# Sample state updates of a retention layer: 32-row stationary tiles replaced by one zero-padded operand of 128 rows

## The chip, the cores and the metric

The kernel runs on one core of a Trainium2 chip. The metric is device time in microseconds (us) of one execution, as the median of several runs. The profile is one execution that was recorded by the hardware profiler; its own time is given beside those of the runs.

## What is computed

The program is one inference step of a two-layer decoder trunk, for 1024 prompt tokens and for 64 sample tokens (8 sequences of 8), which share the weights. Layer 0 mixes tokens by sliding-window attention, layer 1 by retention, a linear attention with a state of 256 x 512 numbers per head and sequence. The change lies in the retention of the sample tokens:

```
def retention_chunk(state, q, k, v, lg):
    ...
    inner = jnp.einsum('bhqs,bshe->bqhe', a, v)
    cross = jnp.einsum('bqhd,bhde->bqhe', q, state) * jnp.exp((idx + 1.0)[:, None] * lg[None])[None, :, :, None]
    k_dec = k * jnp.exp((L - 1.0 - idx)[:, None] * lg[None])[None, :, :, None]
    new_state = jnp.exp(L * lg)[None, :, None, None] * state + jnp.einsum('bshd,bshe->bhde', k_dec, v)
    return new_state, inner + cross
```

For the samples L is 8, there are 8 sequences b and 4 heads h, and `new_state` is an output (`srs`). The last einsum is the state update: for each sequence, head and half of the 256 key rows, a product of 8 tokens deep with 128 x 512 results.

## The kernel before

**Matrix products.** All products run in a type of 32 bits that TensorE takes at reduced precision (`F32R`); where that is not enough, an operand is split into a high and a low part and the product is made as hi x hi, hi x lo and lo x hi. The large projections are made by `mm_t` (L135 to L137, stationary weights, 384 or 320 columns at a time) and `group_n` (L194 to L196, stationary activations, 256 columns). They form a nearly unbroken stream on TensorE. Weights come in slots of 128 x 1024 through a buffer `wraw` (two of them, loaded by SP's queue at L107), and ScalarE and VectorE split them into `whi` and `wlo` (L281, L282).

**Retention of layer 1.** `layer1` weaves the projections with a generator, `ret_units`. It goes through 4 heads x 8 chunks of the prompt. In the round of a chunk stand, one after the other: `ret_mid` of that chunk, `ret_sample_step` with the chunk's number i (0 to 7) as its step, `ret_gate` of the chunk before, `ret_in` of the next chunk, and `ret_sample_load` for the next step. So each head has 8 sample steps. Step i works on the group g = i // 4 of four sequences, on the half k = i // 2 % 2 of the key rows, and on two of the four sequences j (0 and 1 in even steps, 2 and 3 in odd ones).

**The sample's operands.** `ret_sample_in` writes keys and values of a head to two DRAM buffers, `s_kk` and `s_vv`, for each sequence as four blocks of 8 rows: keys hi, hi, lo, lo and values hi, lo, hi, lo. 32 rows of one sequence multiplied with each other so give all four products of the split at once. `ret_sample_load` fetches in even steps four state tiles `s0`, and where k is 0 also the four sequences' keys, as one tile of 128 x 256 from the pool tag `kh1`, and their values, as `vst1` of 128 x 512, one buffer. Both are then used in four steps.

**The update.** `ret_sample_step` makes, for its two sequences, a matmul on the 32 partitions of sequence j (L1080, keys stationary with 32 rows, values moving with 512 columns) into a PSUM buffer `pa` (four in all). VectorE adds the decayed state (L1083) and POOL's queue stores the result (L1084). That makes 4 heads x 8 steps x 2 = 64 such matmuls. In even steps four matmuls come ahead of them for each half (L1069, stationary operands of 128 rows and 32 columns), and in step 0 three with 64 rows (L1072 to L1074).

**What sets the order.** The program's text says what depends on what; the framework replays it in a simulated schedule and writes one list of instructions for each engine, which that engine then takes strictly in turn. Only `weave` with its rates says how densely `ret_units` stands between the projections. SP's queue has the loads, POOL's queue the stores.

Of the kernel before, what the change touches and what calls it, by code (L numbers as in the profile page):

```python
# [9 lines left out]
F32 = mybir.dt.float32  # L10
F32R = mybir.dt.float32r
AF = mybir.ActivationFunctionType
ALU = mybir.AluOpType
# [3 lines left out]
P = 128  # L17
# [36 lines left out]
class Trunk:  # L54
# [795 lines left out]
    def ret_const(self, pool):  # L850
        nc = self.nc
        self.rdec = pool.tile([P, 6, 4], F32, name="rdec", bufs=1)
        nc.sync.dma_start(self.rdec, self.io["rdec"])
        self.qpad = pool.tile([P, 2, 2, 4, 32], F32, name="qpad", bufs=1)
        nc.gpsimd.memset(self.qpad, 0.0)
        self.asamp = [pool.tile([TS, P], F32R, name=f"asamp{i}", bufs=1) for i in range(2)]
        for a in self.asamp:
            nc.gpsimd.memset(a.bitcast(F32), 0.0)
# [181 lines left out]

    def ret_sample_load(self, pool, h, i, u):

        nc = self.nc
        if i % 2:
            return
        g, k = i // 4, i // 2 % 2
        u["s0"] = []
        for j in range(4):
            s0 = pool.tile([P, 512], F32, name="s0", bufs=8)
            nc.sync.dma_start(s0, self.io["st0"][4 * g + j, h, k * P:(k + 1) * P, :])  # L1050
            u["s0"].append(s0)
        if k == 0:
            b = 4 * g
            u["ks"] = pool.tile([P, 256], F32R, name="kh1", bufs=2)
            u["vs"] = pool.tile([P, 512], F32R, name="vst1", bufs=1)
            nc.sync.dma_start(u["ks"].bitcast(F32), self.s_kk[h, b:b + 4].rearrange("b j l c -> (b j l) c"))
            nc.sync.dma_start(u["vs"].bitcast(F32), self.s_vv[h, b:b + 4].rearrange("b j l c -> (b j l) c"))

    def ret_sample_step(self, pool, h, i, u):
        nc = self.nc  # L1060
        mm = nc.tensor.matmul
        gam = 1.0 - 2.0 ** (-5.0 - h)
        g, k = i // 4, i // 2 % 2
        if i == 0:
            u["o"] = self.pa.tile([P, 512], F32, name="pa")
        po = u["o"]
        if i % 2 == 0:
            for j in range(4):
                mm(po[32 * j:32 * j + 32], self.qpad[:, k, g, j], u["s0"][j], start=i == 0, stop=i == 6)  # L1069
        if i == 0:  # L1070
            (ah, al), (vh, vl) = u["a"], u["v"]
            mm(po, ah, vh, start=False, stop=False)  # L1072
            mm(po, ah, vl, start=False, stop=False)
            mm(po, al, vh, start=False, stop=False)  # L1074
        pair = range(i % 2 * 2, i % 2 * 2 + 2)
        pds = {}
        for j in pair:
            pds[j] = self.pa.tile([P, 512], F32, name="pa")
            r = slice(32 * j, 32 * j + 32)
            mm(pds[j], u["ks"][r, k * P:(k + 1) * P], u["vs"][r], start=True, stop=True)  # L1080
        for j in pair:
            s0 = u["s0"][j]
            nc.vector.scalar_tensor_tensor(out=s0, in0=s0, scalar=float(gam ** 8), in1=pds[j], op0=ALU.mult, op1=ALU.add)  # L1083
            nc.gpsimd.dma_start(self.io["srs"][4 * g + j, h, k * P:(k + 1) * P, :], s0)  # L1084
        if i == 7:
            u["on"] = self.groupnorm(pool, po, P, h, 4)
# [257 lines left out]
```

## Time and profile before

| | |
|---|---|
| median of 3 runs | 1697.99 us (1696.72 to 1701.69) |
| profiled execution, own time | 1695.23 us |
| its span | 1693.5 us |
| PE (matmul) busy | 1668.0 us, 98% of the span |
| PEld (weight load) busy | 1583.5 us, 94% |
| DVE (VectorE) busy | 988.7 us, 58% |
| ACT (ScalarE) busy | 612.7 us, 36% |
| POOL (GpSimd) busy | 340.0 us, 20% |
| granted TensorE clock | 0.999 of full speed |

Matmuls are pipelined: the duration of one includes the way through the array, so that the time from start to start says what one takes from the stream, and busy PE is not PE at its peak. A row of the timeline may stand for several instructions (xN) that started together or in one run. The retention's rounds lie between about 690 and 1490 us of the span.

### The profile page before, as it was taken

Reading aid. Unit: us, or ns where it says so; the run is one execution under the profiler, and the core shown is the slowest. Engines: PE = TensorE matmul, PEld = TensorE weight load, DVE = VectorE, ACT = ScalarE, POOL = GpSimd, SP = SyncE. Lnnn points to the kernel's source line nnn. Section 1 sums busy time; section 2 is a strip of 40 time slices with the busy share of each in tenths; the row PEclk is TensorE's granted clock in tenths of the full one; section 3 lists DMA queues with packets and bytes.
Section 4 is the critical chain, followed back from the end, with each engine's and each line's share of the span. In section 5 each row is a group of like instructions: output and inputs, shape, how many; then the busy total and the mean of one; then the engine's idle time right before and its main releaser. Section 6 shows DMA issues by size and latency. Waiting matters only on the chain.

```text
span 1693.5 us, 28264 instructions
## 1 busy us (share of the span) xinstructions
PE 1668.0 (98%) x10600; PEld 1583.5 (94%) x10600; DVE 988.7 (58%) x2184; ACT 612.7 (36%) x1365; POOL 340.0 (20%) x533
## 2 busy tenths in 40 slices
PE   8999999999999999999999999999999999999998
PEld 7989999988999999899999999999899988999998
DVE  7558787966248574246744655455744756443852
ACT  6245555777334341222222312322222432241421
POOL 1413312132001121211123212231122222200000
PEclk9999999999999999999999999999999999999999
DMA  8655646684315443254445544465454865482342
GB/s 288 174 142 154 168 118 170 178 273 166 119 36 173 144 146 119 80 165 154 155 165 183 184 154 160 151 188 177 146 163 146 279 199 172 167 256 86 122 143 87
DMA packets 178697, 273.15 MB, mean 161 GB/s; under 512 B 29968, under 2 KB 128336, under 8 KB 178528
## 3 DMA queue, kind: packets, MB, share of 16 engines
q1 hardware_dynamic: 141152, 177.94, 35.1%
q0 software_dynamic: 37408, 93.40, 15.7%
q8 instruction: 83, 1.36, 0.3%
q14 instruction: 54, 0.44, 0.1%
HBM read 173.45 MB, written 99.68 MB: 161 GB/s over the span
## 4 chain that ended last, share of the span: by engine, by line
PE 73%; issue 1%; DMA 0%; POOL 0%; ACT 0%; DVE 0%; POOLq 0%; ACTq 0%
PE pj L135 17%; PE pj L137 17%; PE pj L136 17%; PE pj L194 3%; PE pj L195 3%; PE pj L196 3%; PE pa L1080 1%; PE pa L1069 1%; PE pa L913 1%; PE pa L1002 1%; PE pa L1003 1%; PE pa L1004 1%; PE pa L944 1%; PE pa L987 1%; PE pa L986 1%
## 5 line engine op out<-in xcount | busy, mean ns | idle before, releaser
L135 PE MATMUL pj<-act,whi 128*128 128x384 f32 (+1 forms) x2160 | 711.9, 330 | 2.3 <-ACT ys L729 1.2
L137 PE MATMUL pj<-act,wlo 128*128 128x384 f32 (+1 forms) x2160 | 707.8, 328 | 0.0
L136 PE MATMUL pj<-act,whi 128*128 128x384 f32 (+1 forms) x2160 | 707.1, 327 | 0.0
L135 PEld LDWEIGHTS pj<-act,whi 128*128 128x128 f32 x2160 | 405.8, 188 | 11.7 <-issue 6.3
L137 PEld LDWEIGHTS pj<-act,wlo 128*128 128x128 f32 x2160 | 405.6, 188 | 4.2 <-issue 3.2
L136 PEld LDWEIGHTS pj<-act,whi 128*128 128x128 f32 x2160 | 405.8, 188 | 3.6 <-issue 2.0
L281 ACT CAST whi<-wraw 128x512 fp32r<-128x512 f32 (+1 forms) x226 | 127.9, 613 | 191.5 <-PE pj L136 150.6
L282 DVE TENSOR_TENSOR wlo<-wraw,whi 128x512 fp32r<-128x512 f32 (+1 forms) x226 | 146.7, 681 | 70.7 <-ACT whi L281 70.3
L194 PE MATMUL pj<-whi,act 128*128 128x256 f32 x528 | 149.0, 286 | 1.1 <-ACT v L871 0.6
L195 PE MATMUL pj<-wlo,act 128*128 128x256 f32 x528 | 148.7, 283 | 0.0
L196 PE MATMUL pj<-whi,act 128*128 128x256 f32 x528 | 147.9, 283 | 0.0
L194 PEld LDWEIGHTS pj<-whi,act 128*128 128x128 f32 x528 | 100.1, 191 | 7.2 <-issue 3.2
L195 PEld LDWEIGHTS pj<-wlo,act 128*128 128x128 f32 x528 | 101.0, 191 | 0.8 <-issue 0.2
L196 PEld LDWEIGHTS pj<-whi,act 128*128 128x128 f32 x528 | 100.6, 191 | 0.3 <-issue 0.2
L518 ACT ACTIVATE s_sb<-s_sb,nm 128x257 f32<-128x257 f32 (+2 forms) x136 | 65.7, 488 | 33.2 <-DVE nm L515 32.6
L871 ACT ACTIVATE v<-pj,rcol 128x256 f32<-128x256 f32 x64 | 29.9, 474 | 127.7 <-PE pj L196 91.7
L330 DVE TENSOR_TENSOR rp_a<-pj,cs 128x768 f32<-128x768 f32 (+1 forms) x39 | 35.6, 912 | 63.5 <-PE pj L137 63.5
L872 POOL DMA_DIRECT2D s_v<-v x64 | 35.4, 554 | 167.8 <-ACT v L871 167.6
L340 DVE TENSOR_TENSOR rp_b<-pj,rbc 128x768 f32<-128x768 f32 (+1 forms) x36 | 32.8, 910 | 50.8 <-PE pj L137 50.7
L959 ACT ACTIVATE kh<-pa,rdec 128x256 fp32r<-128x256 f32 (+1 forms) x36 | 17.0, 473 | 114.0 <-PE pa L956 113.4
L1083 DVE SCALAR_TENSOR_TENSOR s<-s,pa 128x512 f32<-128x512 f32 x64 | 42.2, 684 | 24.5 <-PE pa L1080 24.0
L342 ACT ACTIVATE rp_a<-rp_b 128x768 f32<-128x768 f32 (+1 forms) x36 | 29.2, 810 | 73.1 <-DVE rp_b L340 73.1
(233 smaller groups left out, 2556.6 us busy)
## 6 DMA issues: line engine op xcount, KB each, us to landing
wraw<-wt SPq DMA_DIRECT2D x110, 512.0 KB, 4.4
s<-st SPq DMA_DIRECT2D x64, 256.0 KB, 3.1
srs<-s POOLq DMA_DIRECT2D x64, 256.0 KB, 2.7
act<-s_og SPq DMA_DIRECT2D x48, 192.0 KB, 3.8
qst<-s_q SPq DMA_DIRECT2D x32, 256.0 KB, 4.5
qk<-s_qk SPq DMA_DIRECT2D x32, 256.0 KB, 3.5
s_v<-v POOLq DMA_DIRECT2D x64, 128.0 KB, 2.5
vv<-s_v SPq DMA_DIRECT2D x32, 256.0 KB, 2.7
```

Of the source, the lines that this page charges most:

```text
L135: mm(ps, hi[:, sl], a[c][:, 0], start=start and i == 0, stop=False)
L136: mm(ps, hi[:, sl], a[c][:, 1], start=False, stop=False)
L137: mm(ps, lo[:, sl], a[c][:, 0], start=False, stop=stop and i == last)
L194: mm(o, hi, w[0][:, sl], start=start, stop=False)
L195: mm(o, hi, w[1][:, sl], start=False, stop=False)
L196: mm(o, lo, w[0][:, sl], start=False, stop=stop)
L281: self.nc.scalar.copy(hi, x)
L282: self.nc.vector.tensor_tensor(out=lo, in0=x, in1=hi.bitcast(F32), op=ALU.subtract)
L330: nc.vector.tensor_tensor(out=ta, in0=ps, in1=self.cs[:, 0:1, c0:c0 + n].broadcast_to([P, 2, n]), op=ALU.mult)
L518: nc.scalar.activation(s[:, h, :], s[:, h, :], AF.Exp, bias=nm[:, h, :], scale=0.125, accum_out=den[:, h:h + 1])
L872: nc.gpsimd.dma_start(self.s_v1[h, i, :, g * 256:g * 256 + 256], st)
L1083: nc.vector.scalar_tensor_tensor(out=s0, in0=s0, scalar=float(gam ** 8), in1=pds[j], op0=ALU.mult, op1=ALU.add)
```

## The change

Two lines make a tile `kpad` of four slots, 128 rows by 128 columns each, and fill it with zeros once, at the start of layer 1. Slot j receives the 32 rows of sequence j on its own partitions 32j to 32j+31; the other 96 rows stay zero. The matmul then takes the whole slot as stationary operand and all 128 rows of `vs`: rows of other sequences meet zeros. The keys are no longer loaded as one tile of 256 columns for two halves but as four loads of 32 x 128 in every even step. There is one `kpad`, so a load into a slot has to follow the matmul that read it last. The matmuls of a step are no longer written ahead of the two VectorE operations but in turn with them.

```diff
@@ ret_const
         nc.gpsimd.memset(self.qpad, 0.0)
+        self.kpad = pool.tile([P, 4, P], F32R, name="kpad", bufs=1)
+        nc.gpsimd.memset(self.kpad.bitcast(F32), 0.0)
         self.asamp = [pool.tile([TS, P], F32R, name=f"asamp{i}", bufs=1) for i in range(2)]
@@ ret_sample_load
             u["s0"].append(s0)
+        b = 4 * g
+        for j in range(4):
+            nc.sync.dma_start(self.kpad[32 * j:32 * j + 32, j].bitcast(F32),
+                              self.s_kk[h, b + j, :, :, k * P:(k + 1) * P].rearrange("j l c -> (j l) c"))
         if k == 0:
-            b = 4 * g
-            u["ks"] = pool.tile([P, 256], F32R, name="kh1", bufs=2)
             u["vs"] = pool.tile([P, 512], F32R, name="vst1", bufs=1)
-            nc.sync.dma_start(u["ks"].bitcast(F32), self.s_kk[h, b:b + 4].rearrange("b j l c -> (b j l) c"))
             nc.sync.dma_start(u["vs"].bitcast(F32), self.s_vv[h, b:b + 4].rearrange("b j l c -> (b j l) c"))
@@ ret_sample_step
-        pair = range(i % 2 * 2, i % 2 * 2 + 2)
-        pds = {}
-        for j in pair:
-            pds[j] = self.pa.tile([P, 512], F32, name="pa")
-            r = slice(32 * j, 32 * j + 32)
-            mm(pds[j], u["ks"][r, k * P:(k + 1) * P], u["vs"][r], start=True, stop=True)
-        for j in pair:
+        for j in range(i % 2 * 2, i % 2 * 2 + 2):
+            pd = self.pa.tile([P, 512], F32, name="pa")
+            mm(pd, self.kpad[:, j], u["vs"], start=True, stop=True)
             s0 = u["s0"][j]
-            nc.vector.scalar_tensor_tensor(out=s0, in0=s0, scalar=float(gam ** 8), in1=pds[j], op0=ALU.mult, op1=ALU.add)
+            nc.vector.scalar_tensor_tensor(out=s0, in0=s0, scalar=float(gam ** 8), in1=pd, op0=ALU.mult, op1=ALU.add)
             nc.gpsimd.dma_start(self.io["srs"][4 * g + j, h, k * P:(k + 1) * P, :], s0)
```

On SP's queue the loads stand in the order of the schedule. The first place is the start of head 0, behind the load of its values (`vst`); the lines of the changed kernel are two to four higher (vst L1057 is now L1061, vv L926 is L928, s L1050 is L1053). Before:

```order
L1057 DMA vst_8315<-s_vv 128x512
L107 DMA wraw<-wt 128x1024
L926 DMA vv_9039<-s_v_89 128x512
L1050 DMA s_9239<-st 128x512
L107 DMA wraw<-wt 128x1024
L1050 DMA s_9241<-st 128x512
```

Now:

```order
L1061 DMA vst_8320<-s_vv 128x512
L1057 DMA kpad<-s_kk 32x128 x2
L107 DMA wraw<-wt 128x1024
L928 DMA vv_9047<-s_v_89 128x512
L1053 DMA s_9247<-st 128x512
L107 DMA wraw<-wt 128x1024
```

Two loads into slots 0 and 1, for step 2, stand ahead of the weights; they have to follow the two matmuls of step 0. Each head has such loads in pairs: four loads at its start, that follow no matmul of their own head, and six pairs behind steps 0 to 5.

The second place is in head 2, around two loads of weights. Before:

```order
L931 DMA sgl<-s_sg_90 128x4x128
L107 DMA wraw<-wt 128x1024 x2
L1050 DMA s_12451<-st 128x512
L924 DMA qk_12141<-s_qk_88 128x4x128
L1050 DMA s_12453<-st 128x512
```

Now:

```order
L933 DMA sgl<-s_sg_90 128x4x128
L1057 DMA kpad<-s_kk 32x128
L107 DMA wraw<-wt 128x1024
L1057 DMA kpad<-s_kk 32x128
L107 DMA wraw<-wt 128x1024
L1053 DMA s_12477<-st 128x512
```

Here each load of weights stands behind a load into `kpad`. On PE the 64 matmuls of the update stand where they stood, but for a few that moved by some matmuls of the projections.

## Rows read from the trace of the kernel before

**Rows 1.** Busy time by engine, 690 to 1490 us (x instructions, clock, DMA share, GB/s).

```profile
690.00:1490.00 800.00, 796.88 (x5035) 732.99 (x5034) 433.12 (x831) 218.81 (x441) 184.08 (x285) 1.00 0.52 170
```

**Rows 2.** Instructions of line 1080 (ns min/median/max, first and last start), whole span.

```profile
L1080 PE MATMUL pa<-vst,kh x64: 489/497/501, 745.3 to 1470.3; 32*128 32x512 f32 x64
L1080 PEldq EVENT_SEMAPHORE  x8: 51/51/933, 743.0 to 1418.2; - x8
```

**Rows 3.** Timeline of PE, a lone update (start, duration; stationary rows*columns, moving shape).

```profile
972.49 0.33 PE L136 MATMUL pj<-act,whi 128*128 128x384 f32 x1
...
973.01 0.34 PE L136 MATMUL pj<-act,whi 128*128 128x384 f32 x1
973.28 0.49 PE L1080 MATMUL pa<-vst,kh 32*128 32x512 f32 x1
973.70 0.44 PE L137 MATMUL pj<-act,wlo 128*128 128x384 f32 x1
973.97 0.34 PE L135 MATMUL pj<-act,whi 128*128 128x384 f32 x1
```

**Rows 4.** Timeline of PE, 512 columns with 128 stationary rows.

```profile
1285.76 0.40 PE L1004 MATMUL pa<-vh,kl 128*128 128x512 f32 x1
...
1286.46 0.40 PE L1004 MATMUL pa<-vh,kl 128*128 128x512 f32 x1
```

**Rows 5.** Timeline of PE, two updates started together.

```profile
820.93 0.34 PE L137 MATMUL pj<-act,wlo 128*128 128x384 f32 x1
821.20 0.50 PE L1080 MATMUL pa<-vst,kh 32*128 32x512 f32 x2
821.63 0.44 PE L135 MATMUL pj<-act,whi 128*128 128x384 f32 x1
821.91 0.34 PE L136 MATMUL pj<-act,whi 128*128 128x384 f32 x1
```

**Rows 6.** Timeline of PE, matmuls of 32 columns with and without updates behind them.

```profile
795.49 1.06 PE L1069 MATMUL pa<-s,qpad 128*32 128x512 f32 x8
796.48 0.50 PE L1080 MATMUL pa<-vst,kh 32*128 32x512 f32 x2
...
797.20 0.34 PE L136 MATMUL pj<-act,whi 128*128 128x384 f32 x1
...
1195.25 1.07 PE L1069 MATMUL pa<-s,qpad 128*32 128x512 f32 x8
...
1196.53 0.34 PE L136 MATMUL pj<-act,whi 128*128 128x384 f32 x1
```

**Rows 7.** Waits of the weight loads, 690 to 1490 us (us in total, times, longest).

```profile
PEld pa L1080 <- issue: 8.1, 28, 0.8
```

**Rows 8.** Matmuls with 64 stationary rows (line by form, ns min/median/max).

```profile
L1072 PE MATMUL pa<-vh,asamp x4: 493/493/497, 744.4 to 1343.7; 64*128 64x512 f32 x4
L1073 PE MATMUL pa<-vl,asamp x4: 383/392/393, 744.7 to 1344.0; 64*128 64x512 f32 x4
```

**Rows 9.** Waits of SP's queue, 600 to 1500 us (us in total, times, longest).

```profile
SPq L1057 <- PE pa L1080: 11.1, 4, 3.4
```

**Rows 10.** Timeline of SP's queue and of ACT: loads of weights and a split.

```profile
740.36 0.32 SPq L1057 DMA_DIRECT2D vst<-s_vv  x1
747.11 0.33 SPq L107 DMA_DIRECT2D wraw<-wt  x1
...
909.75 0.33 SPq L107 DMA_DIRECT2D wraw<-wt  x1
...
931.15 0.61 ACT L281 CAST whi<-wraw 128x512 fp32r<-128x512 f32 x1
```

**Rows 11.** Landing of the eight loads of keys (line 1056).

```profile
DMA to landing us min/median/max: 1.9/3.2/4.8
```

**Rows 12.** Timeline of POOL at the start of layer 1.

```profile
622.07 0.60 POOL L855 MEMSET qpad<- 128x512 f32 x1 [2.77 <-DMA s_x<-ys]
...
625.40 1.19 POOL L239 TENSOR_TENSOR rcol<-nv,mhalf 128x3 f32<-128x3 f32 x1 [2.16 <-DVE nv L238]
```

## The prediction

> **What bounds the kernel now.** I first looked at the busy time of each engine in the stretch in which the update runs. Between 690 and 1490 us PE is busy for 796.9 of 800 us at the full granted clock, VectorE for 433 and ScalarE for 219 [rows 1]. So TensorE sets the pace there, and whatever the stream of matmuls loses or gains goes straight into the time. Busy PE does not mean that the array does useful work all the time, though, so the next view is the timeline of PE, where the distance from start to start says what a matmul takes out of the stream. The rows to look for are the 64 updates of L1080 [rows 2]. I went through all of them along the timeline: they stand in 48 groups, 32 lone ones and 16 pairs that start together.
>
> A lone update in the middle of the projections [rows 3]: the matmuls of 384 columns ahead of it follow each other at 0.173 us (972.49 to 973.01, three steps). From the last of these to the second one behind the update, 973.01 to 973.97, it takes 0.96 us. Two steps of 0.173 us belong to the projection, so the update takes 0.61 us out of the stream. The same 512 columns with 128 stationary rows follow each other at 0.233 us (1285.76 to 1286.46, three steps) [rows 4]. So about 0.38 us of each lone update is not its work but a gap. It stands on both sides: the update starts 0.27 us after its neighbour in place of 0.17, and the projection behind it needs 0.27 us to the next start in place of 0.17.
>
> A pair takes 0.98 us in the same way (820.93 to 821.91), so 0.63 us for two [rows 5]: the second update comes free.
>
> What makes the gap? The same picture shows where 64 stationary rows come in: the first matmul of that form lasts 493 ns, the next, of the same form, 392 [rows 8]. And behind the matmuls of 32 stationary columns the stream also needs longer, 1.28 us from their start to the second projection [rows 6]. The gap appears wherever the tile's form changes, and not between matmuls of one form. The weight loads of L1080 wait 28 times, 8.1 us in all, for nothing that the profile shows [rows 7], which is how a gap inside TensorE would look.
>
> **The change, part by part.**
>
> The matmuls. With 128 stationary rows the update has the form of its neighbours, and I price it at 0.233 us like the other matmuls of 512 columns [rows 4]. By groups:
> - 28 lone updates with projections on both sides: 28 x 0.38 = 10.8 us gained.
> - 6 pairs with projections on both sides: before 0.63 us, after 2 x 0.233 = 0.47, so 6 x 0.17 = 1.0 us gained.
> - 10 pairs that touch another form (32 columns, 64 rows, transposes). Behind matmuls of 32 columns, from their start to the second projection, it is 1.71 us with the pair (795.49 to 797.20); without updates it is 1.28 [rows 6]. After the change it would be 1.28 + 0.47 = 1.75: nothing gained, since the change of form stays with the neighbour. I take 0 for all ten; at best each gains like a pure pair (+1.7 us), at worst each loses the 0.04 just worked out (-0.4 us).
> - 4 lone updates that touch another form: a lone one takes as long as a pair, so 1.71 - (1.28 + 0.23) = 0.20 us each behind the 32 columns, and at most 0.38 each. I take 0.28: 1.1 us gained.
>
> Sum: 10.8 + 1.0 + 1.1 = 12.9 us gained, between 11.2 and 15.0.
>
> One more semaphore per matmul. Each update now waits for a load of its own beside its PSUM buffer. Before, eight updates had an extra semaphore instruction of 51 ns on PE's queue [rows 2]; now up to 56 more may have one, 2.9 us at most. I take nothing, because the queue runs it while the array still works on the 0.17 us of the projection ahead; the 2.9 us go into the range.
>
> The loads. 64 loads of 32x128 numbers take the place of 8 of 128x256: the same bytes. Issuing takes 0.32 us each by the neighbouring load of SP's queue [rows 10], so 56 x 0.32 = 18 us more on a queue that has 800 us. What can hurt is their waiting: 24 pairs of them must follow updates that read the same slots, and what stands behind them on SP (weights, `vv`, `qk`, `sgl`, `s0`) waits along. Before, the load of values at L1057 already waited for L1080 four times, 11.1 us in all, 3.4 at the longest [rows 9]. At the first place shown, the values go out at 740.36 and the weights at 747.11, which is behind the first update at 745.3 anyway [rows 2, 10]: the two loads fit in between. Weights have cover: one that is issued at 909.75 is split at 931.15, 21 us later [rows 10]. If a wait outlasted that, the stall would be its length less those 21 us. A slot is reloaded for the update two steps later; landing takes 1.9 to 4.8 us by the loads of the keys [rows 11], and two steps are some 50 us in the first head (the updates of steps 0 and 2 start at 745 and 796 us [rows 2, 6]). I cost loads and waits at nothing.
>
> VectorE and stores. The two additions of a step are the same and their PSUM buffers come a little sooner or later; VectorE is busy for little over half of the stretch [rows 1]. Nothing.
>
> The fill with zeros. One more memset of 128x512 on POOL, 0.60 us, stands ahead of a small operation at 625.40 that first waits 2.16 us for VectorE [rows 12]. It is hidden; its price without that cover is 0.6 us, once.
>
> The profiled execution took 1695.2 us (span 1693.5), and less 12.9 that is 1682.3. The median of the runs, 1698.0, is 2.8 us above it; on that scale I predict **1685 us**.
>
> **The rivals.**
>
> *The gaps stay.* The gap might belong to waiting, for a free PSUM buffer or for the semaphore, and not to the tile's form. Then the lone updates keep their 0.61 us, and the 16 pairs lose that the second one comes free: 16 x 0.233 = 3.7 us more, 1702 us, within what a measurement can tell from no change (0.3%, 5 us). For it: most of these matmuls do wait for a PSUM buffer's reader by the program's text, so form and wait come together. Against it: the 64-row matmuls show the same step, and 28 of the waits are put down to nothing [rows 7, 8]. Chance 0.06. The Trainium skill, "TensorE: Matmul & The Clock Gate", section "Why this matters for your kernels", speaks for this side: it advises small contractions to be put on distinct 32-row groups because such matmuls then run at the same time. By that advice alone the sum would be the +3.7 us of this rival; the trace agrees that pairs share their time (0.63 us for two [rows 5]), but it also shows the gap, which is larger.
>
> *SP is held up, and the kernel gets slower.* If the schedule's order does not fit the chip's pace, a `kpad` load sits at SP's head until its update is done, and the weights, `vv` or `qk` behind it come late. To turn 12.9 us of gain into a loss of over 5, the stalls have to reach 18 us: 0.75 us at each of the 24 pairs of waiting loads. At twice that, 36 us, it would be 1698 - 12.9 + 36 = 1721 us. For it: at the second place each load of weights stands behind such a wait. Against it: waits behind L1080 were 3.4 us at the longest [rows 9], weights have 21 us of cover [rows 10], and `s0`, behind most of these pairs, has to wait for a later event of the same step. Chance 0.03.
>
> *Half is given back.* A few updates wait for their slot, or the semaphore shows, or neighbouring gaps grow: 3 to 8 us of stall, 1688 to 1693 us, still faster. Chance 0.16, of which 0.04 ends within 0.3%.
>
> **How the numbers follow.** The forecast has 0.75. The range: at the low end 1698.0 - 15.0 = 1683, less 3 because the profiled execution was that much below the median, 1680. At the high end 1698.0 - 11.2 + 2.9 = 1690, and 2 more for part of the third rival, 1692. Faster by over 0.3%: 0.75 + 0.12 = 0.87; within 0.3%: 0.06 + 0.04 = 0.10; slower: 0.03.
>
> **What would show it.** In the profile after: L1080's line (now L1081) with 128*128 and a median near 390 ns in place of 497; starts of 0.17, 0.23 and 0.17 us around a lone update; PE still busy for all but a few us of the stretch, which is some 13 us shorter; no wait of PE for `kpad`. I am wrong if the starts around the 128-row update stay at 0.27 and 0.43 us (the form is not the cause), or if PE shows new waits for loads, or SP long waits for PE with late weights behind them.

## The result and the profile after

| | before | after |
|---|---|---|
| median of 4 runs | 1698.94 us (1696.72 to 1701.69) | 1687.53 us (1682.10 to 1689.55) |
| profiled execution, own time | 1695.23 us | 1686.98 us |
| its span | 1693.5 us | 1685.2 us |
| PE busy | 1668.0 us | 1657.9 us |
| PEld busy | 1583.5 us | 1589.8 us |

The ratio of the times is 0.9927, with a 95% interval from 0.9899 to 0.9955: 11.4 us by the medians, between 7.6 and 17 us by the interval. So the kernel is faster, by 0.7%, and the time lies 2.5 us above the forecast of 1685 us, inside its range of 1680 to 1692.

The stretch of the update first: busy time by engine from 690 to 1490 us, as in [rows 1].

```profile
690.00:1490.00 800.00, 796.13 (x5120) 748.80 (x5121) 437.98 (x844) 226.33 (x457) 186.53 (x289) 1.00 0.54 173
```

PE is as busy as before and at the same clock, but it gets through 5120 matmuls in the 800 us in place of 5035. The gain does not show in PE's busy share; it shows in how much work fits under the same share. The busy time of the weight loads (PEld, the second pair of figures) does show it: 748.8 us in place of 733.0. The instructions of the update, now line 1081, answer to [rows 2]:

```profile
L1081 PE MATMUL pa<-vst,kpad x64: 389/394/504, 747.9 to 1463.2; 128*128 128x512 f32 x64
L1081 PEldq EVENT_SEMAPHORE  x61: 51/51/51, 745.4 to 1460.1; - x61
```

The median falls from 497 to 394 ns. The timeline of PE shows what that means in the stream. A lone update, as in [rows 3]:

```profile
974.12 0.34 PE L136 MATMUL pj<-act,whi 128*128 128x384 f32 x1
974.30 0.39 PE L1081 MATMUL pa<-vst,kpad 128*128 128x512 f32 x1
974.53 0.33 PE L137 MATMUL pj<-act,wlo 128*128 128x384 f32 x1
974.70 0.34 PE L135 MATMUL pj<-act,whi 128*128 128x384 f32 x1
```

From start to start 0.18, 0.23 and 0.17 us, where it was 0.27, 0.42 and 0.27. And a pair, as in [rows 5]:

```profile
822.79 0.34 PE L137 MATMUL pj<-act,wlo 128*128 128x384 f32 x1
822.96 0.62 PE L1081 MATMUL pa<-vst,kpad 128*128 128x512 f32 x2
823.42 0.33 PE L135 MATMUL pj<-act,whi 128*128 128x384 f32 x1
823.60 0.34 PE L136 MATMUL pj<-act,whi 128*128 128x384 f32 x1
```

The two updates now come one after the other, 0.46 us for both, and the gaps around them are gone: 0.81 us in place of 0.98. Behind matmuls of 32 columns, the pair of [rows 6] gains nothing:

```profile
797.33 1.06 PE L1073 MATMUL pa<-s,qpad 128*32 128x512 f32 x8
798.32 0.73 PE L1081 MATMUL pa<-vst,kpad 128*128 128x512 f32 x2
798.88 0.33 PE L135 MATMUL pj<-act,whi 128*128 128x384 f32 x1
799.06 0.34 PE L136 MATMUL pj<-act,whi 128*128 128x384 f32 x1
```

797.33 to 799.06 is 1.73 us, before it was 1.71.

**A measure that does not scatter.** Executions of one and the same kernel differ by several us, and the profiles show where: the first update starts at 745.27 us in the profile before, and at 747.86, 750.44 and 756.66 in three profiles of the changed kernel, because PE waits now longer, now shorter ahead of it: up to 740 us the second of these three has a wait of 5.8 us for a load of weights (L567), the third one of 8.7 us for ScalarE (L605), and the first none as long at either line. From the first update to the last matmul of the program the same work stands in the profiles of both kernels (5896 matmuls), the granted clock is 1.00 from 757 to 1675 us in all of them, and this time hardly scatters. The timeline of PE, first update and last matmul of the kernel before:

```profile
745.27 0.50 PE L1080 MATMUL pa<-vst,kh 32*128 32x512 f32 x2
...
1688.48 0.31 PE L137 MATMUL pj<-act,wlo 128*128 128x320 f32 x1
```

That is 943.21 us. The same rows of the kernel after:

```profile
747.86 0.73 PE L1081 MATMUL pa<-vst,kpad 128*128 128x512 f32 x2
...
1680.19 0.31 PE L137 MATMUL pj<-act,wlo 128*128 128x320 f32 x1
```

932.33 us: 10.9 less, while the spans differ by 8.3, since the first update happened to come 2.6 us later. Below I call this time, first start of an update to the last start of a matmul, the tail.

### The profile page after: what moved, and what is told of

Its sections match the earlier page's. It is cut to its first block, busy times and chain, and to the rows that moved or that the text cites. A ratio compares the mean times of both kernels' runs of the same rounds, so it can differ in the third digit from the quotient of the medians.

```text
span 1685.2 us, 28410 instructions
## 1 busy us (share of the span) xinstructions
PE 1657.9 (98%) x10600; PEld 1589.8 (94%) x10600; DVE 986.9 (59%) x2184; ACT 612.4 (36%) x1365; POOL 340.0 (20%) x534
## 4 chain that ended last, share of the span: by engine, by line
PE 70%; issue 2%; DMA 1%; POOL 1%; ACT 0%; DVE 0%; POOLq 0%; ACTq 0%; DVEq 0%
PE pj L135 16%; PE pj L137 16%; PE pj L136 16%; PE pj L194 3%; PE pj L195 3%; PE pj L196 3%; PE pa L1073 1%; PE pa L1081 1%; PE pa L1004 1%; PE pa L1005 1%; PE pa L1006 1%; PE pa L946 1%; PE pa L915 1%; PE pa L987 1%; PE pa L988 1%
## 5 line engine op out<-in xcount | busy, mean ns | idle before, releaser
L651 POOL DMA_DIRECT2D s_og<-og x40 | 29.0, 724 | 124.5 <-DVE og L650 99.7
```

## The experiments

Theory: TensorE leaves a gap when the form of the tile changes between neighbouring matmuls (stationary rows and columns), 0.38 us in all around a lone update, and the padding takes that change away. Rivals: the gain came with something else that the change brought (buffers, loads, the turn of matmul and addition); the gap goes with the number of rows; the gap belongs to each 32-row matmul and not to the change of form. The table gives each run with its ratio to the kernel before, as timed beside it (medians of 1698.45 to 1698.94 us).

| run | median, us | ratio to before (95%) | first update, last matmul | tail, us |
|---|---|---|---|---|
| before | | | 745.27, 1688.48 | 943.21 |
| after | 1687.53 | 0.9927 (0.9899 to 0.9955) | 747.86, 1680.19 | 932.33 |
| e0_again (after) | 1688.35 | 0.9942 (0.9920 to 0.9964) | 750.44, 1681.58 | 931.14 |
| e9_after_beside (after) | 1687.62 | 0.9935 (0.9914 to 0.9957) | 756.66, 1687.81 | 931.15 |
| e1_loads_only | 1699.56 | 1.0005 (0.9993 to 1.0017) | 748.73, 1693.02 | 944.29 |
| e2_rows64 | 1702.45 | 1.0028 (1.0014 to 1.0041) | 753.26, 1700.81 | 947.55 |
| e3_even_only | 1696.11 | 0.9987 (0.9970 to 1.0004) | 744.12, 1683.25 | 939.13 |
| e5_turn_only | 1700.14 | 1.0010 (0.9993 to 1.0026) | 748.02, 1691.24 | 943.22 |
| e6_twice_32 | 1710.49 | 1.0062 (1.0039 to 1.0085) | 751.05, 1704.72 | 953.67 |
| e7_twice_128 | 1701.14 | 1.0014 (1.0001 to 1.0028) | 750.33, 1693.87 | 943.54 |
| e4_two_kpads | 1687.74 | 0.9933 (0.9913 to 0.9953) | 748.34, 1678.31 | 929.97 |
| e8_one_state_load | 1685.91 | 0.9922 (0.9900 to 0.9944) | 746.63, 1675.99 | 929.36 |

**The changed kernel again.** 

> The changed kernel once more, beside its neighbours of this group. Every theory: 1687 us within 3, 0.9927 of the kernel before. Of use for the scatter, and for the small losses outside the updates (3 us in the first profile): if they belong to the order of the work they are there again, if to chance they are not.

1688.35 us, ratio 0.9942. The tail is 931.14 us, 1.2 less than in the first profile of the same kernel. What was different there is one wait of PE (waits of PE, 740 to 1475 us, kernel after):

```profile
PE pa L1004 <- DVE sgl L1098: 0.9, 1, 0.9
```

The state's matmul waited for VectorE, which waited for a load of `sgl`. The repetition has no such wait in that stretch, nor has the third profile (e9_after_beside), although both keep the same order of matmuls. So the wait belonged to that execution.

**All of the change but the form.**

```diff
-            mm(pd, self.kpad[:, j], u["vs"], start=True, stop=True)
+            r = slice(32 * j, 32 * j + 32)
+            mm(pd, self.kpad[r, j], u["vs"][r], start=True, stop=True)
```

> All of the change but the form: kpad, its zeros, its 64 loads and their semaphores stay, the matmul uses the 32 rows of its sequence alone, stationary and moving. If the form of the tile makes the gap: the whole gain goes, 1699 us within 3, a lone update takes 0.61 us out of the stream again, a pair 0.63. If the gain came with something else that the change brought (a buffer of kh1 that is free for the prompt's keys, the loads, the turn of matmul and addition): it stays near 1687 us and a lone update near 0.23.

1699.56 us, no different from before, and the tail is 944.29 us. A lone update in the timeline of PE:

```profile
976.48 0.34 PE L136 MATMUL pj<-act,whi 128*128 128x384 f32 x1
976.74 0.49 PE L1082 MATMUL pa<-vst,kpad 32*128 32x512 f32 x1
977.16 0.44 PE L137 MATMUL pj<-act,wlo 128*128 128x384 f32 x1
977.44 0.34 PE L135 MATMUL pj<-act,whi 128*128 128x384 f32 x1
```

0.96 us from 976.48 to 977.44, as in [rows 3], with all loads, zeros and semaphores of the change in place. What these cost can be read at the first update of the last head, when three of the four heads have passed. The timeline of PE, kernel before:

```profile
1344.60 0.50 PE L1080 MATMUL pa<-vst,kh 32*128 32x512 f32 x2
```

This run:

```profile
1348.07 0.50 PE L1082 MATMUL pa<-vst,kpad 32*128 32x512 f32 x2
```

From the first update of the program it is 599.33 us (from 745.27) and 599.34 (from 748.73). So over these 599 us the loads, their waits and the semaphores cost nothing; the 1.1 us by which the whole tail is longer arise behind this point, where the order of the matmuls differs (see the run with one load of states). The whole gain is in the form. The changed kernel differs from this run in nothing else, and its 5896 matmuls stand in the same order; against this run the padding is worth 944.29 - 931.14 = 13.2 us of the tail.

**64 rows.**

```diff
-            mm(pd, self.kpad[:, j], u["vs"], start=True, stop=True)
+            r = slice(64 * (j // 2), 64 * (j // 2) + 64)
+            mm(pd, self.kpad[r, j], u["vs"][r], start=True, stop=True)
```

> Half the padding: stationary and moving operand are the 64 rows that hold sequence j and its neighbour, zeros in the neighbour's. If any form other than that of the neighbouring matmuls makes the gap: a lone update still takes 0.61 us, and a pair, now on the same 64 rows, no longer runs together and takes 0.61 + 0.23 = 0.84, so 16 x 0.2 = 3.4 us more than before, 1702 us. If the gap goes with the number of rows: about 0.42 us for a lone one and some 1694 us.

1702.45 us, ratio 1.0028; the tail is 3.3 us longer than with 32 rows in the same place (947.55 - 944.29), the 3.4 of the first reading. The timeline of PE, a lone update:

```profile
982.70 0.34 PE L136 MATMUL pj<-act,whi 128*128 128x384 f32 x1
982.97 0.50 PE L1082 MATMUL pa<-vst,kpad 64*128 64x512 f32 x1
983.40 0.44 PE L137 MATMUL pj<-act,wlo 128*128 128x384 f32 x1
983.67 0.34 PE L135 MATMUL pj<-act,whi 128*128 128x384 f32 x1
```

0.97 us: the gap is as large with 64 rows as with 32, so the number of rows does not make it. And a place where the neighbour ahead has 64 rows too:

```profile
753.03 0.39 PE L1078 MATMUL pa<-vh,asamp 64*128 64x512 f32 x1
753.26 0.62 PE L1082 MATMUL pa<-vst,kpad 64*128 64x512 f32 x2
753.81 0.41 PE L135 MATMUL pj<-act,whi 128*128 128x320 f32 x1
```

Here the update starts 0.23 us after its neighbour, without a gap. In the changed kernel, whose update has 128 rows, the same step takes 0.32 us, from this matmul to the first update at 747.86:

```profile
747.54 0.39 PE L1078 MATMUL pa<-vh,asamp 64*128 64x512 f32 x1
```

Padding to 128 rows makes the gap at this neighbour, where 64 rows avoid it. So it is the difference between neighbours that counts. (The gap on the other side, to the projections, stays with 64 rows, so that this place as a whole gains nothing.)

**Even steps alone.**

```diff
-            mm(pd, self.kpad[:, j], u["vs"], start=True, stop=True)
+            r = slice(32 * j, 32 * j + 32) if i % 2 else slice(0, P)
+            mm(pd, self.kpad[r, j], u["vs"][r], start=True, stop=True)
```

> Padding to 128 rows in even steps alone, 32 rows in odd ones. If the form makes the gap, the gain splits by groups: summed over the groups of the trace before, even steps hold 5.2 us of it and odd ones 8.0, so 1694 us within 3; updates of even steps take 0.23 us, lone ones of odd steps 0.61, in one and the same run. If the gain came with anything that both kinds of step share (loads, buffers): 1687 us and one price for both.

The median, 1696.11 us, lies between the two kernels, 2 us above the first reading and, by its interval, not clear of the kernel before. The tail is sharper: 944.29 - 939.13 = 5.2 us gained over the run without padding, just the 5.2 that the groups of the even steps held. Both prices stand in one timeline, first an update of an even step, then one of an odd step:

```profile
1193.93 0.34 PE L136 MATMUL pj<-act,whi 128*128 128x384 f32 x1
1194.10 0.39 PE L1082 MATMUL pa<-vst,kpad 128*128 128x512 f32 x1
1194.34 0.33 PE L137 MATMUL pj<-act,wlo 128*128 128x384 f32 x1
...
1215.21 0.31 PE L135 MATMUL pj<-act,whi 128*128 128x320 f32 x1
1215.45 0.50 PE L1082 MATMUL pa<-vst,kpad 32*128 32x512 f32 x1
1215.88 0.41 PE L136 MATMUL pj<-act,whi 128*128 128x320 f32 x1
1216.13 0.31 PE L137 MATMUL pj<-act,wlo 128*128 128x320 f32 x1
```

**Each 32-row update twice.**

```diff
-            mm(pds[j], u["ks"][r, k * P:(k + 1) * P], u["vs"][r], start=True, stop=True)
+            for _ in range(2):
+                mm(pds[j], u["ks"][r, k * P:(k + 1) * P], u["vs"][r], start=True, stop=True)
```

> The kernel before, each 32-row update made twice into the same buffer. If the gap is paid for each change of form: the second one of a lone update costs only its own 0.23 us, one of a pair between 0.2 and 0.46 in all, so 32 x 0.23 + 16 x 0.2 to 0.46 = 11 to 15 us more, 1710 to 1714 us. If each 32-row matmul carries the gap: 0.61 us for each second one, 48 x 0.61 = 29 us more, 1728 us.

1710.49 us; the tail grows by 10.5 us, a little under the 11 of the theory and far from 29. The order moved too: four lone updates now stand as two pairs (46 groups in place of 48), and the matmuls of 32 columns stand in 20 runs in place of 19. By the prices of this document these two nearly cancel (about 1.2 us less and 1.1 more). Two in a row, in the timeline of PE:

```profile
980.21 0.34 PE L136 MATMUL pj<-act,whi 128*128 128x384 f32 x1
980.48 0.73 PE L1081 MATMUL pa<-vst,kh 32*128 32x512 f32 x2
981.14 0.44 PE L137 MATMUL pj<-act,wlo 128*128 128x384 f32 x1
981.41 0.33 PE L135 MATMUL pj<-act,whi 128*128 128x384 f32 x1
```

980.21 to 981.41 is 1.20 us, 0.24 more than with one. The second 32-row matmul costs its own columns and no more: the gap is paid for going into another form and out of it, and not once more for a second matmul in between.

**Each padded update twice.**

```diff
-            mm(pd, self.kpad[:, j], u["vs"], start=True, stop=True)
+            for _ in range(2):
+                mm(pd, self.kpad[:, j], u["vs"], start=True, stop=True)
```

> The changed kernel, each padded update made twice. It measures the price of 0.233 us by itself: 64 x 0.233 = 15 us more than the changed kernel, 1702 us.

1701.14 us, but the tail grows by only 943.54 - 931.14 = 12.4 us. The order of this kernel has 18 runs of the matmuls of 32 columns in place of 20 (counted along the timeline), and what such a run costs is the subject of the run with one load of states; with 1.1 us for each the sum is 14.6. So the price is confirmed only with that correction.

**Two kpads.**

```diff
-        self.kpad = pool.tile([P, 4, P], F32R, name="kpad", bufs=1)
-        nc.gpsimd.memset(self.kpad.bitcast(F32), 0.0)
+        self.kpads = [pool.tile([P, 4, P], F32R, name=f"kpad{i}", bufs=1) for i in range(2)]
+        for t in self.kpads:
+            nc.gpsimd.memset(t.bitcast(F32), 0.0)
...
-            mm(pd, self.kpad[:, j], u["vs"], start=True, stop=True)
+            mm(pd, self.kpads[k][:, j], u["vs"], start=True, stop=True)
```

> The changed kernel with a kpad for each half of the key rows, so that a load follows the update four steps back and not two. The waits of SP's queue for the update (95.7 us, 28 times in the profile after) should nearly go. If they cost PE nothing: the time stays, 1687 us within 3. If they made part of the 3 us that were lost outside the updates: 1684 to 1686 us and no wait of PE in the stretch beyond those of the kernel before.

The wait of SP's queue for the update, in the kernel after (us in total, times, longest):

```profile
SPq L1057 <- PE pa L1081: 95.7, 28, 14.0
```

With two kpads:

```profile
SPq L1058 <- PE pa L1082: 26.4, 16, 5.4
```

The waits for the update fall by 69 us and the time stays: 1687.74 us against 1687.53, 1688.35 and 1687.62. The tail is 1.2 us shorter than in the two later profiles of the changed kernel, but this order also has one run of the 32-column matmuls less (19 in place of 20), and that accounts for it. The queue does not wait less, though. The loads of states wait longer for the stores of the states before them, in the kernel after and with two kpads:

```profile
SPq L1053 <- DMA srs<-s: 120.3, 47, 13.4
SPq L1054 <- DMA srs<-s: 149.3, 47, 17.3
```

Summed over all rows of that view, 740 to 1475 us, SP's queue waits 626 us in the kernel before, 596 in the kernel after and 601 with two kpads. A wait that is taken away is waited somewhere else, so this run shows that it does not matter for what the queue waits; that the waits cost nothing is shown by the first 599 us of the run without padding, in which SP waited 88.5 us for the update.

**The turn alone.** The kernel before, with its loop over the pair written as in the change (a matmul, its addition, its store, then the next).

> The kernel before, with only the turn of matmul and addition as the change has it. If it moves nothing: 1699 us within 3, 48 groups, 16 of them pairs, 0.61 and 0.63 us. If the turn breaks pairs up: each costs up to 0.6 us more, up to 1708 us; if the turn was part of the gain, below 1695 us.

1700.14 us, and a tail of 943.22 us against 943.21, with the same order of matmuls. The turn moves nothing.

**The four states in one load.** On top of the two kpads:

```diff
-        u["s0"] = []
-        for j in range(4):
-            s0 = pool.tile([P, 512], F32, name="s0", bufs=8)
-            nc.sync.dma_start(s0, self.io["st0"][4 * g + j, h, k * P:(k + 1) * P, :])
-            u["s0"].append(s0)
+        s0 = pool.tile([P, 4, 512], F32, name="s0", bufs=2)
+        nc.sync.dma_start(s0, self.io["st0"][4 * g:4 * g + 4, h, k * P:(k + 1) * P, :].rearrange("b p e -> p b e"))
+        u["s0"] = [s0[:, j] for j in range(4)]
```

> Two kpads, and the four state tiles of a load made one tile with one DMA, so that the four matmuls that read them (32 stationary columns, L1069 before) stand together more often: 18 runs of them on PE in place of 20. If each split of such a run costs a change of form, about 1.3 us (0.98 + 0.34 us in the profile after, at 1390.20 and 1391.18): 2.6 us less than the changed kernel, some 1685 us, and from the first update to the last some 711 us in place of 714 to 715. If splits cost nothing: as with two kpads alone, 713 us and 1688. If the larger load comes too late: PE waits for it, over 1690 us.

> The changed kernel once more, as the neighbour of the run before on the same chip: 1688 us within 3, from the first update to the last 714 to 715 us.

1685.91 us against 1687.62 of the changed kernel beside it; the intervals of the two ratios (0.9900 to 0.9944 and 0.9914 to 0.9957) overlap, so the times alone do not show that it is better. The tail, 929.36 us, is 1.8 us shorter than 931.15, in the direction of the reading with splits but less than its 2.6, and only 0.6 us shorter than with two kpads, which has one run more. About 0.3 us of it was lost at 889 us, where a weight load waited for ScalarE. By the measure of the expectation, first to last update, it is 711.4 us against 714.1, so 2.7 less, but that stretch holds five matmuls fewer (4561 in place of 4566) and so flatters the run. What a split costs can be read in the kernel after, where the order puts other matmuls into a run of L1073 (L1069 before):

```profile
1390.20 1.04 PE L1073 MATMUL pa<-s,qpad 128*32 128x512 f32 x2
1391.18 0.50 PE L987 MATMUL pa<-Sh,qh 128*128 128x512 f32 x1
...
1392.77 1.06 PE L1073 MATMUL pa<-s,qpad 128*32 128x512 f32 x6
1393.76 0.44 PE L135 MATMUL pj<-act,whi 128*128 128x384 f32 x1
```

A run of two takes 0.98 us, a run of six or eight 0.99: the four column groups share their time only while they stand together. The kernel before has 19 such runs and the changed one 20. The changed kernel has the order of the run without padding, whose tail is 1.1 us longer than before (944.29 against 943.21). That, the 1.2 us of the two kpads and the 0.9 of this run without its wait put one run at about 1 us; these orders differ in some other neighbours as well, so the price is an estimate.

## Why the prediction was right

*What bounds the kernel.* TensorE did, and it still does: the tail fell by about what the stream of matmuls lost in gaps.

*The matmuls, 12.9 us (11.2 to 15.0).* Against the run that differs in the form alone the padding is worth 13.2 us. The parts came out as worked out: lone updates take 0.23 us in place of 0.61, pairs 0.46 in place of 0.63, and the pair behind 32 columns gains nothing (1.73 against 1.71, forecast 1.75). The sum has three flaws that do not change its end. 28 x 0.38 is 10.6 and not 10.8, so that the sum is 12.7. The low end of 11.2 leaves out the 1.0 of the six pairs; with it, the parts as written give 12.2. And the nothing for the ten pairs is right as a sum only: a transpose has 128 x 128 like the projections, so the three pairs ahead of transposes gain 0.11 to 0.12 us each, and the seven beside 32 columns or 64 rows lose 0.02 to 0.08 each. Against the kernel before, the tail is 12.1 us shorter in two of three profiles and 10.9 in the first; 1.1 us went to a step that the prediction did not have, a split run in the new order of PE. Of the 2.5 us by which the measured time lies above 1685 us, 0.95 come from the median of the kernel before, from which the forecast counted: it was 1697.99 us of three runs and is 1698.94 with the fourth. The rest is about the size of the split run, and within the scatter of the runs.

*The extra semaphore, nothing.* 61 of the 64 updates now have an extra semaphore instruction of 51 ns, and the starts around them are 0.17 to 0.18 us all the same. The run without padding has 61 as well and loses nothing over 599 us. It is hidden.

*The loads, nothing.* At the first place of the order SP issued as was read from it, the two loads behind the first update and the weights behind them (timeline of SP's queue, kernel after):

```profile
742.82 0.32 SPq L1061 DMA_DIRECT2D vst<-s_vv  x1
748.39 0.86 SPq L1057 DMA_DIRECT2D kpad<-s_kk  x2
749.71 0.35 SPq L107 DMA_DIRECT2D wraw<-wt  x1
```

Elsewhere the waits were far longer than the 3.4 us that [rows 9] suggested: 14.0 us at the longest and 95.7 in all. So one sign of being wrong, long waits of SP for PE, came true in its first half; the weights behind them did not come late. The load of [rows 10] goes out at 911.18 in the kernel after and is split at 932.46, 21.3 us later, as before. The cover was there, and the waits were not short. It was smaller than the prediction took it, since loads of weights need about 4 us of it to land (4.5 by the page of the profile); the 14.0 us still fit. For `vv`, `qk` and `sgl` no run measures the cover by itself; the run without padding shows only that their waits cost PE nothing there. That argument against the slower rival was right in its end and wrong in one of its numbers.

*The zeros, nothing.* The memset stands where it was expected, and the operation behind it still waits for VectorE and not for POOL (timeline of POOL, kernel after):

```profile
627.04 0.67 POOL L857 MEMSET kpad<- 128x512 f32 x1
...
630.16 1.19 POOL L239 TENSOR_TENSOR rcol<-nv,mhalf 128x3 f32<-128x3 f32 x1 [1.87 <-DVE nv L238]
```

*The rivals.* "The gaps stay" is excluded from both sides: with 128 rows and 61 semaphores there is no gap, and with 32 rows and the same 61 semaphores it is there. The advice that it cited, from the Trainium skill, "TensorE: Matmul & The Clock Gate", section "Why this matters for your kernels", holds for what it says: pairs on distinct 32-row groups did run together, and in the 64-row run, where they share a group, 3.3 us of that were lost. Its price for this kernel is outweighed by the change of form. That change is named in the Trainium skill's "TensorEngine Tiling (Array Packing)", section "Tiling Modes": changing the mode drains the engine. The traces agree in that a change of form costs time, and they give it a number, 0.38 us for a lone update there and back; what TensorE does in that time they do not show. "SP is held up" did not come about, as told. Of "half is given back", 1.1 us came true, by the order and not by waits. The medians (1687.5 to 1688.4 us) lie at the lower edge of its 1688 to 1693 us, so the times alone would not tell it from the forecast; the tail does.

## What to carry to other kernels

A matmul on fewer rows was not cheaper here than one on 128, and between matmuls of another form it cost a gap on both sides, 0.38 us on top of 0.23. Padding with zeros pays when such matmuls stand alone among full tiles, and two that run together are still too few here (0.63 us against 0.46). Behind matmuls of 32 columns or 64 rows padding a pair gained nothing, because the change of form stays. PE's busy share does not show such gaps (796.9 and 796.1 of 800 us). The busy time of the weight loads does (733.0 and 748.8), and the distances from start to start say where they are. Where executions scatter by more than the gain, look for two points in the trace between which the same work stands: the tail agreed to 0.01 us in two of three profiles of the changed kernel, whose times differed by several us, and the third had a wait of its own. And a wait that disappears from a queue may only have moved: add up all waits before calling it saved.

## What was not expected of the hardware

The gap is the same for 32 and for 64 rows (0.96 us around 32 rows, 0.97 around 64), and it vanishes beside a neighbour of the same form (0.23 us from start to start behind a 64-row matmul, 0.32 where the form changes). Four matmuls of 32 columns take as long as one: 0.99 us for the run of eight instructions, 0.98 for the run of two; splitting such a run costs about 1 us. And a queue may wait long without any loss: of the 735 us from 740 to 1475 SP waited 626 in the kernel before and 596 in the changed one, and 88.5 us of new waits for the update left the 599 us of the run without padding where they were.
